# Two PSUM banks for the filling projections of a dilated attention, an earlier first conditioning sum, and layer 1 projections emitted between attention heads

## The chip, the cores and the metric

The kernel runs on one core of a Trainium2 chip. Its time is the device time of one execution in microseconds (us); lower is better. The kernel before was timed in three runs: 3086.98, 3095.9 and 3100.1 us, median 3095.9 us. The profile is of another execution, which took 3091.59 us.

## The reference, cut to what matters

A two-layer encoder works on 2048 tokens of width 1024 in float32. Layer 0 mixes tokens with a dilated window attention (A, 8 heads of 64) beside a differential attention over all tokens (B, 4 heads of 2 x 64); layer 1 uses a banded attention with grouped keys (C, 16 query heads on 4 key heads). Each layer has a silu gate path and an output projection, and its norm is shifted and scaled by sums over the conditioning vector `c`.

```
cs = silu(c)
for layer in range(2):
    shift, scale, gate = split(cs @ ada_w[layer] + ada_b[layer], 3)
    h = rms_norm(x, norm_g[layer]) * (1 + scale) + shift
    if layer == 0:
        qa, ka, va, qb, kb, vb, g = split(h @ ab_w_in)
        ya = dilated_mixture_attention(qa, ka, va)   # (window, dilation): (128,1), (512,4), (2048,16)
        yb = differential_attention(qb, kb, vb)      # softmax1 - lam*softmax2, all 2048 keys
        y = (concat(ya, yb) * silu(g)) @ ab_w_out
    else:
        q, k, v, g = split(h @ c_w_in)
        y = (banded_attention(q, k, v, half_window=128, sink) * silu(g)) @ c_w_out
    x = x + gate * y
return rms_norm(x, final_g)
```

## The kernel before, in words

Every float32 product of a projection is made of three fp32r matmuls: both operands are split into a high and a low part, and high x high, high x low and low x high are summed in one PSUM bank (`three`, L271). One piece of a projection (`proj_pieces`, L310) is 128 output columns for a block of 512 tokens, 24 such matmuls of 128x512. Its weights come in by one DMA, ScalarE and then VectorE or GpSimd split them (L319, L320), and a sink reads the finished bank: for the gates ScalarE takes a tanh (L385), VectorE multiplies (L387), and a DMA stores the result (`sink_gate`, L382).

The stages in the program's order are these. `layer0_proj` (L427) sums the products of `ada_w` with the conditioning vector (`ada_acc`, L152: eight products on VectorE for each of four sums `acc_ss`; four small matmuls with `ones` add up the partitions, L200), norms x, and makes q, k and v of B. `diff_attention` (L542) runs the four heads B0 to B3, and the projections of A stand in the program behind them. `dilated_attention` (L669) runs eight heads A0 to A7 in pairs; each head has a natural half (scores `pqn`, transposes `ptn`, output `pyn`) and a half by residue classes (`pqc`, `ptc`, `pyc`), and after each pair its two patterns are combined (`dil_combine`, L893: the factors are transposed into `pf`, L911, go to DRAM and come back broadcast as `F`, L922). Beside these heads a generator of 32 gate pieces (`layer0_gate_proj`, L537, tile `pp_g0` in bank `mm` of the pool `psG`) is advanced at every second `tick` (L719). `layer0_out` (L1010) multiplies attention and gate and projects; the part called 0b (L1197, tokens 768 to 1791, the upper half of the contraction) takes its tiles from `psG` too, the full part starts at L1209 in the pool `psO`. Layer 1 follows: `layer1_norm` and `layer1_qkv` for a block of 512 tokens, `attend` (L1092) for each of 16 tiles t of 128 queries (scores `pqC`, transposes `ptC`, output `pyC`), 32 gate pieces (`layer1_gate`, L1062, `pp_g1`), the output.

PSUM has eight banks in this plan. During the dilated heads `psG` holds one, `psA` holds s=2, t=3, y=2.

No queue is written by hand. The framework's scheduler sets the order of each engine's instructions before the program runs, from the program's order, the buffers that a tile may use and its own estimates of durations; so a piece that the program names late can stand early on an engine if its buffers are free, and the order is fixed on the chip.

## Time and profile before

| | |
|---|---|
| median of 3 runs | 3095.9 us (3086.98 to 3100.1) |
| profiled execution | 3091.59 us |
| its span | 3089.5 us |
| TensorE (PE) busy | 2789.2 us, 90% of the span |
| VectorE (DVE) busy | 1908.3 us, 62% |
| ScalarE (ACT) busy | 1490.5 us, 48% |
| GpSimd (POOL) busy | 1140.2 us, 37% |
| mean granted TensorE clock | 0.96 of 2.4 GHz |
| DMA | 593.78 MB, 192 GB/s |

The busy times are of one execution on the chip. A busy TensorE is a sum over the modelled ends of pipelined matmuls; how far apart two matmuls start says more. The granted clock is a mean over a stretch of the two levels 1.2 and 2.4 GHz, 1.00 being the upper one.

### The profile page before, as it was taken

The page shows a single profiled execution, that of the slowest core. Times are in us where ns is not written, and L with a number is a line of the kernel's source. Part 1 is how long each engine was busy: PE and PEld are TensorE (multiplying, and loading weights), DVE is VectorE, ACT ScalarE, POOL GpSimd, SP SyncE. Part 2 cuts the span into 40 slices and gives each one's busy share as a digit, 9 for nine tenths or more (in the row PEclk, how much of TensorE's full clock was granted, in tenths as well). Part 3 has the DMA queues.
Part 4 walks back from the last instruction along what each step waited for, and adds up shares of the span by engine and source line. Part 5 has one row for each costly group of instructions (what it writes and reads, how often), then busy time and mean ns, then how long its engine had stood idle before and what let it go on. Part 6 is the DMA issues. An engine that isn't in the chain of part 4 may idle for free. (4 is left out here: it accounts for less than half of the span.)

```text
span 3089.5 us, 43710 instructions
## 1 busy us (share of the span) xinstructions
PE 2789.2 (90%) x14992; PEld 2340.6 (76%) x14992; DVE 1908.3 (62%) x4128; ACT 1490.5 (48%) x2841; POOL 1140.2 (37%) x755
## 2 busy tenths in 40 slices
PE   4999899999999999998778885899888999999898
PEld 3788778888888888876666774788777778887687
DVE  7425286777677676657676665354565676565476
ACT  4311255555555555536666562122565576565321
POOL 3200075555655654312433432132333353333221
PEclk8999999999999999999889998999989999999999
DMA  6587743653654552357778986586988678885654
GB/s 261 207 297 233 206 137 110 188 174 112 169 157 159 152 167 86 133 169 203 179 197 214 254 225 195 189 289 196 254 203 228 182 177 209 215 220 180 206 196 160
DMA packets 554552, 593.78 MB, mean 192 GB/s; under 512 B 32257, under 2 KB 421594, under 8 KB 548186
## 3 DMA queue, kind: packets, MB, share of 16 engines
q1 hardware_dynamic: 542490, 574.21, 64.2%
q10 hardware_dynamic: 11840, 16.78, 1.7%
q8 instruction: 119, 1.95, 0.3%
q14 instruction: 103, 0.84, 0.1%
HBM read 414.36 MB, written 176.46 MB: 191 GB/s over the span
## 5 line engine op out<-in xcount | busy, mean ns | idle before, releaser
L615 ACT ACTIVATE s<-s,nm 128x2048 f32<-128x2048 f32 x128 | 257.0, 2008 | 170.3 <-DVE nm L614 170.2
L621 POOL TENSOR_SCALAR s<-s,rr 128x1536 f32<-128x1536 f32 x64 | 125.2, 1956 | 364.2 <-DVE rr L619 265.6
L564 PE MATMUL pq<-kB,q 128*128 128x512 f32 x512 | 215.9, 422 | 30.0 <-DMA kB<-kB 14.0
L1124 DVE CUSTOM_DVE_ANT_0 sC<-pqC,tabC,isl 128x384 f32<-128x384 f32 (+1 forms) x256 | 148.3, 597 | 134.5 <-PE pqC L565 91.7
L624 POOL TENSOR_TENSOR s<-s,s 128x1536 f32<-128x1536 f32 x64 | 229.0, 3579 | 4.8
L636 ACT ACTIVATE th<-pt 128x512 fp32r<-128x512 f32 x256 | 146.2, 596 | 171.0 <-PE pt L632 138.2
L609 DVE CUSTOM_DVE_ANT_0 s<-pq,ndist 128x1024 f32<-128x1024 f32 x128 | 156.0, 1219 | 93.4 <-PE pq L565 65.7
L565 PE MATMUL pq<-kB,q 128*128 128x512 f32 x512 | 206.5, 403 | 0.0
L637 DVE TENSOR_TENSOR tl<-pt,th 128x512 fp32r<-128x512 f32 x256 | 169.3, 682 | 55.8 <-ACT th L636 55.6
L609 DVE CUSTOM_DVE_ANT_0 s<-pq,ndist,mx 128x1024 f32<-128x1024 f32 x128 | 163.4, 1276 | 28.8 <-PE pq L565 26.8
L1132 ACT ACTIVATE sC<-sC,nmC 128x384 f32<-128x384 f32 (+1 forms) x256 | 151.6, 595 | 57.4 <-DVE nmC L1129 57.0
L276 PE MATMUL py<-tl,vB 128*128 128x256 f32 x512 | 150.2, 293 | 7.8 <-DVE tl L637 7.8
L632 PE MATMUL pt<-ident,s 128*128 128x128 f32 x1024 | 149.9, 275 | 0.0
L273 PE MATMUL py<-th,vB 128*128 128x256 f32 x512 | 147.1, 287 | 1.8 <-ACT th L636 1.7
L277 PE MATMUL py<-th,vB 128*128 128x256 f32 x512 | 145.3, 284 | 0.0
L564 PEld LDWEIGHTS pq<-kB,q 128*128 128x128 f32 x512 | 98.7, 193 | 59.6 <-DVE mx L609 23.6
L1138 PE MATMUL ptC<-ident,sC 128*128 128x128 f32 x736 | 136.4, 282 | 3.4 <-ACT sC L1132 3.4
L967 POOL TENSOR_TENSOR yr<-yr,gr 128x512 f32<-128x512 f32 (+1 forms) x46 | 58.0, 1262 | 214.6 <-DMA yr<-yT 56.9
L277 PE MATMUL pp_l<-h1T,wt_l 128*128 128x512 f32 x320 | 127.7, 401 | 8.6 <-POOL wt_l L320 6.5
L1145 POOL TENSOR_SCALAR hC<-rC 128x512 fp32r<-128x512 f32 x64 | 41.4, 646 | 239.2 <-ACT rC L1144 195.1
L273 PE MATMUL pp_l<-h1T,wt_l 128*128 128x512 f32 x320 | 127.7, 400 | 0.1
L276 PE MATMUL pp_l<-h1T,wt_l 128*128 128x512 f32 x320 | 127.3, 399 | 0.0
(415 smaller groups left out, 9118.3 us busy)
## 6 DMA issues: line engine op xcount, KB each, us to landing
wr_a<-in_ab_w_in_dram SPq DMA_DIRECT2D x48, 512.0 KB
wr_l<-in_c_w_in_dram SPq DMA_DIRECT2D x48, 512.0 KB
hD<-h0T SPq DMA_DIRECT2D x8, 2048.0 KB
aw_ss<-in_ada_w_dram SPq DMA_DIRECT2D x32, 512.0 KB
hs_a<-hD SPq DMA_DIRECT2D x16, 1024.0 KB
q<-qB SPq DMA_DIRECT2D x128, 128.0 KB
wr_g<-in_ab_w_in_dram SPq DMA_DIRECT2D x32, 512.0 KB
hs_g<-hD SPq DMA_DIRECT2D x16, 1024.0 KB
```

Source lines behind the costliest of these rows:

```text
L273: first = nc.tensor.matmul(pt, l[0], r[0], start=(k == 0), stop=False)
L276: nc.tensor.matmul(pt, l[0], r[1], start=False, stop=False)
L277: nc.tensor.matmul(pt, l[1], r[0], start=False, stop=(k == nk - 1))
L564: first = nc.tensor.matmul(ps_, q0, k0, start=True, stop=False)
L565: nc.tensor.matmul(ps_, q1, k1, start=False, stop=True)
L609: nc.vector.tensor_tensor_reduce(out=s_[:, half * 1024:(half + 1) * 1024], in0=pq, in1=ndist[:, o:o + 1024], scale=1.0, scalar=LOW if half ...
L615: nc.scalar.activation(s_, s_, AF.Exp, bias=nm, scale=slope_B(h), accum_out=lsum[:, a, t:t + 1])
L624: nc.gpsimd.tensor_tensor(Pm[0][:, W:], Pm[0][:, W:], Pm[1][:, W:], op=OP.add)
L632: nc.tensor.transpose(pt[:, kk, j], A[j][:, kb * P:(kb + 1) * P], ident)
L637: nc.vector.tensor_tensor(lo, src, f32(hi), op=OP.subtract)
L1124: nc.vector.tensor_tensor_reduce(out=s_[:, :n], in0=pq[:, :n], in1=tab[:, o:o + n], scale=1.0, scalar=isl[:, h:h + 1], op0=OP.add, op1=OP.max,
L1132: nc.scalar.activation(Sx[r][:, :n], Sx[r][:, :n], AF.Exp, bias=nm[:, h:h + 1], scale=slope_C(h), accum_out=ls[:, h:h + 1])
```

## The change

There are three edits.

1. A class `Turns` hands out tiles from several pools, one after the other. The gate pieces of the dilated attention and part 0b of the output take their tiles in turn from `psG` and from a new pool `psF` of one bank, which is opened with the pools of A. The transposes of A have two banks, not three.
2. Of the eight products of each first conditioning sum, the third and fourth (`OWN`) are no longer made on VectorE: TensorE multiplies the raw weight columns by the conditioning values and adds them in the bank that sums the partitions. The load of `ada1_1` is issued ahead of the first weights of q.
3. In layer 1 `layer1_qkv` of the next block and 24 of the 32 gate pieces are generators now, advanced inside `attend` after each group of four heads; the norm of the next block stands ahead of the attends instead of behind them. The last eight gate pieces follow after the attends as before, behind the last scores.

```diff
+class Turns:
+    def __init__(self, *pools):
+        self.pools, self.n = pools, 0
+    def tile(self, *args, **kw):
+        self.n += 1
+        return self.pools[self.n % len(self.pools)].tile(*args, **kw)
...
+    OWN = (2, 3)
...
             for k in range(KC):
-                add(acc, raw[:, k], k)
+                if k not in OWN:
+                    add(acc, raw[:, k], k)
...
-            for f in range(4):
-                nc.tensor.matmul(pc[:, f:f + 1], accs[i, j][:, f * P:(f + 1) * P], ones[:, 0:1], start=True, stop=True)
+            terms = [(accs[i, j], ones[:, 0:1])]
+            if raw is not None:
+                terms = [(raw[i][j][:, k], cs[:, k:k + 1]) for k in OWN] + terms
+            for n, (a, b) in enumerate(terms):
+                for f in range(4):
+                    nc.tensor.matmul(pc[:, f:f + 1], a[:, f * P:(f + 1) * P], b, start=(n == 0 and f == 0),
+                                     stop=(n == len(terms) - 1), skip_group_check=True)
...
             ada_load(raw, 0, 0)
+            ada_load(raw, 0, 1, (1,))
             w0 = load_w(pool, ab_w_in, 1536, CH, "qb0", "wt", nc.gpsimd)
-            ada_load(raw, 0, 1)
+            ada_load(raw, 0, 1, (0,))
...
-        ps = Bufs(ps_, s=2, t=3, y=2)
+        ps = Bufs(ps_, s=2, t=2, y=2)
...
-        dilated_attention(pool_A, pool_AC, ps_A, fill, psG)
+        psG2 = Turns(psG, Bufs(with_A.enter_context(psum("psF", side="right")), mm=1))
+        dilated_attention(pool_A, pool_AC, ps_A, fill, psG2)
...
-        layer0_out(pool, psG, w, [upper], g, x, x0d, "0b", "mm", range(FULL, HALF))
+        layer0_out(pool, psG2, w, [upper], g, x, x0d, "0b", "mm", range(FULL, HALF))
...
+            ts = range(max(4 * b - 1, 0), 4 * b + 3 if b < TB - 1 else NT)
             if b + 1 < TB:
                 h1 = layer1_norm(pj, psj, b + 1)
-                layer1_qkv(pj, psj, h1, b + 1, qs)
+                between, n = layer1_qkv(pj, psj, h1, b + 1, qs), 14
+            else:
+                between, n = chain(*(layer1_gate(pj, psj, h1 if g == TB - 1 else None, g)
+                                     for g in (TB - 1, *range(TB - 2)))), 8 * (TB - 1)
+            at = [0, 0]
+            def tick():
+                at[0] += 1
+                while at[1] * len(ts) * C_KV < at[0] * n:
+                    at[1] += 1
+                    next(between, None)
+            for t in ts:
+                last = attend(pool, ps, t, V, consts, tick)
+            for _ in between:
+                pass
```

The order of the engines moves with it at three places. The first is ScalarE late in the last differential head, B3; `th3_6` are its copies of transposed scores of query pair 6, `s3_14` and `s3_15` the exponentials of tiles 14 and 15, `th_g0` the tanh of a gate piece and `wt_g0` the split of its weights. Before:

```order
L615 ACTIVATE s3_15_0_9628,l3_8116<-s3_15_0_9628,nm3_15_0_9642 128x2048
L385 ACTIVATE th_g04_1_14755<-pp_g0_1_4_14730 128x512
L319 ACTIVATE wt_g0_1_6_15109<-wr_g0_1_6_15107 128x1024
L641 ACTIVATE yB3_8115<-py3_5_9247 128x256
L636 ACTIVATE th3_6_0_9467<-pt3_6_0_9462 128x512
L645 ACTIVATE sq3_2_9369<-yB3_8115 128x512
L636 ACTIVATE th3_6_1_9482<-pt3_6_1_9477 128x512
L615 ACTIVATE s3_15_1_9645,l3_8116<-s3_15_1_9645,nm3_15_1_9659 128x2048
L649 ACTIVATE row3_2_9373<-pr3_2_9371 1x512
L385 ACTIVATE th_g05_1_14916<-pp_g0_1_5_14891 128x512
L319 ACTIVATE wt_g0_1_7_15314<-wr_g0_1_7_15312 128x1024
```

and now:

```order
L658 ACTIVATE th3_6_0_9491<-pt3_6_0_9486 128x512
L658 ACTIVATE th3_6_1_9506<-pt3_6_1_9501 128x512
L637 ACTIVATE s3_14_0_9612,l3_8140<-s3_14_0_9612,nm3_14_0_9626 128x2048
L671 ACTIVATE row3_2_9397<-pr3_2_9395 1x512
L637 ACTIVATE s3_14_1_9629,l3_8140<-s3_14_1_9629,nm3_14_1_9643 128x2048
L658 ACTIVATE th3_6_2_9521<-pt3_6_2_9516 128x512
L658 ACTIVATE th3_6_3_9536<-pt3_6_3_9531 128x512
L637 ACTIVATE s3_15_0_9652,l3_8140<-s3_15_0_9652,nm3_15_0_9666 128x2048
L658 ACTIVATE th3_6_4_9551<-pt3_6_4_9546 128x512
L658 ACTIVATE th3_6_5_9566<-pt3_6_5_9561 128x512
L637 ACTIVATE s3_15_1_9669,l3_8140<-s3_15_1_9669,nm3_15_1_9683 128x2048
```

The gate pieces are gone from this place. In the whole program 480 of the 768 gate matmuls of layer 0 stood ahead of the first dilated score on TensorE, and 48 do now; the other 720 stand in the dilated heads A0 to A3 (A2's class half has none), where before the heads A0 to A7 held 288, most of them from A5's class half on.

The second is TensorE at the end of the last dilated pair; `pyc7` and `ptc7` are of head A7, `pf3` is the transpose of the last combining factors, `po0b_6_1` the second half of output tile 6 of part 0b. Before:

```order
L277 MATMUL po0b_6_1_18575<-woh0b_18540,yl0b_6_4_18582 128x512
L875 MATMUL pyc7_3_18392<-cl7_3_2_18410,vc7_3_18366 128x512
L875 MATMUL pyc7_3_18392<-ch7_3_0_18419,vc7_3_18366 128x384
L875 MATMUL pyc7_3_18392<-cl7_3_0_18420,vc7_3_18366 128x384
L911 MATMUL pf3_18491<-ident_110,M3_18477 64x128
L875 MATMUL pyc7_3_18392<-ch7_3_3_18431,vc7_3_18366 128x384
L875 MATMUL pyc7_3_18392<-cl7_3_3_18432,vc7_3_18366 128x384
L273 MATMUL po0b_7_0_18618<-woh0b_18540,yh0b_7_4_18625 128x512
L276 MATMUL po0b_7_0_18618<-wol0b_18541,yh0b_7_4_18625 128x512
L277 MATMUL po0b_7_0_18618<-woh0b_18540,yl0b_7_4_18626 128x512
```

and now:

```order
L294 MATMUL po0b_10_0_18771<-woh0b_18567,yh0b_10_4_18778 128x512
L897 MATMUL pyc7_3_18419<-cl7_3_2_18437,vc7_3_18393 128x512
L883 MATMUL ptc7_3_3_18454<-ident_110,scl7_3_1_18402 128x128
L883 MATMUL ptc7_3_3_18454<-ident_110,scl7_3_2_18408 128x128
L883 MATMUL ptc7_3_3_18454<-ident_110,scl7_3_3_18414 128x128
L297 MATMUL po0b_10_0_18771<-wol0b_18568,yh0b_10_4_18778 128x512
L298 MATMUL po0b_10_0_18771<-woh0b_18567,yl0b_10_4_18779 128x512
L933 MATMUL pf3_18518<-ident_110,M3_18504 64x128
L294 MATMUL po0b_10_1_18772<-woh0b_18567,yh0b_10_4_18778 128x512
L297 MATMUL po0b_10_1_18772<-wol0b_18568,yh0b_10_4_18778 128x512
```

Ahead of `pf3` stood 24 of the 192 matmuls of part 0b, the tile 6; now 108 do, the tiles 6 to 9 and half of 10.

The third is TensorE at the start of the last attend of layer 1, t = 15; `pp_g1_1_7` is the last piece of gate block 1. Before:

```order
L1138 MATMUL ptC15_0_15_26855<-ident_110,sC15_0_26821 128x128
L1138 MATMUL ptC15_0_15_26855<-ident_110,sC15_1_26826 128x128
L1138 MATMUL ptC15_0_15_26855<-ident_110,sC15_2_26831 128x128
L1138 MATMUL ptC15_0_15_26855<-ident_110,sC15_3_26836 128x128
L273 MATMUL pp_g1_1_7_27950<-h1G1_0_5_27673,wt_g1_1_7_27947 128x512
L276 MATMUL pp_g1_1_7_27950<-h1G1_1_5_27681,wt_g1_1_7_27947 128x512
L1151 MATMUL pyC15_0_26843<-hC15_0_14_26849,vC_14_26223 128x512
L277 MATMUL pp_g1_1_7_27950<-h1G1_0_5_27673,wt_g1_1_7_27947 128x512
L273 MATMUL pp_g1_1_7_27950<-h1G1_0_6_27674,wt_g1_1_7_27947 128x512
```

and now:

```order
L1160 MATMUL ptC15_0_15_27647<-ident_110,sC15_0_27613 128x128
L1160 MATMUL ptC15_0_15_27647<-ident_110,sC15_1_27618 128x128
L1160 MATMUL ptC15_0_15_27647<-ident_110,sC15_2_27623 128x128
L1160 MATMUL ptC15_0_15_27647<-ident_110,sC15_3_27628 128x128
L1173 MATMUL pyC15_0_27635<-hC15_0_14_27641,vC_14_26633 128x512
L1173 MATMUL pyC15_0_27635<-lC15_0_14_27642,vC_14_26633 128x512
L586 MATMUL pqC15_8_27788<-khC15_27597,qC_15_27599 128x256
L587 MATMUL pqC15_8_27788<-klC15_27598,qC_15_27599 128x256
L586 MATMUL pqC15_9_27793<-khC15_27597,qC_15_27599 128x256
L587 MATMUL pqC15_9_27793<-klC15_27598,qC_15_27599 128x256
```

The pieces that the program lets run here have ended before: about a quarter of t = 14's and all of t = 15's attention matmuls, some 100, now stand without gate matmuls between them, and the last eight pieces follow the last scores as before.

## Rows read from the trace of the kernel before

**Rows 1.** the page: busy time by engine, and the granted clock in 40 slices.

```profile
PE 2789.2 (90%) x14992; PEld 2340.6 (76%) x14992; DVE 1908.3 (62%) x4128; ACT 1490.5 (48%) x2841; POOL 1140.2 (37%) x755
...
PEclk8999999999999999999889998999989999999999
```

**Rows 2.** busy time by engine in nine stretches of layer 0.

```profile
core 0: us, PE busy (x) PEld busy (x) DVE busy (x) ACT busy (x) POOL busy (x), PEclk, DMA share, GB/s
1181.60:1242.80 61.20, 61.20 (x345) 52.35 (x345) 41.21 (x76) 33.68 (x47) 26.95 (x10) 1.00 0.28 80
1242.80:1375.50 132.70, 125.60 (x679) 104.65 (x678) 73.96 (x136) 58.32 (x85) 44.03 (x20) 0.99 0.47 152
1451.20:1476.60 25.40, 21.18 (x120) 17.43 (x118) 17.57 (x55) 16.90 (x42) 6.09 (x8) 0.93 0.71 182
1476.60:1510.00 33.40, 21.68 (x129) 17.81 (x129) 20.84 (x66) 19.61 (x55) 15.46 (x15) 0.88 0.73 183
1510.00:1536.10 26.10, 20.78 (x108) 16.55 (x107) 18.95 (x47) 19.54 (x50) 14.85 (x16) 0.89 0.67 173
1674.70:1710.20 35.50, 32.96 (x174) 27.34 (x173) 20.20 (x58) 20.40 (x48) 9.96 (x11) 1.00 0.90 262
1710.20:1752.40 42.20, 36.66 (x198) 30.90 (x199) 28.92 (x71) 24.88 (x60) 11.60 (x10) 0.92 0.93 254
1752.40:1802.00 49.60, 44.67 (x209) 35.31 (x208) 28.63 (x56) 26.07 (x60) 30.07 (x26) 0.93 0.82 212
1868.20:1947.10 78.90, 43.97 (x153) 31.86 (x151) 38.01 (x49) 11.31 (x15) 11.55 (x7) 0.85 0.73 213
```

**Rows 3.** TensorE's timeline: gate matmuls back to back, first and fifth.

```profile
1342.64 0.39 PE L276 MATMUL pp_g<-hs_g,wt_g 128*128 128x512 f32 x1
...
1343.55 0.39 PE L277 MATMUL pp_g<-hs_g,wt_g 128*128 128x512 f32 x1
```

**Rows 4.** groups by line of VectorE between 1181.6 and 1242.8 us.

```profile
L320 DVE TENSOR_TENSOR wt_g<-wr_g,wt_g 128x1024 fp32r<-128x1024 f32 x3 | 3.7, 1223 | 0.3 <-ACT wt_g L319 0.3
L387 DVE SCALAR_TENSOR_TENSOR gg_g<-th_g,pp_g 128x512 f32<-128x512 f32 x5 | 3.4, 684 | 4.5 <-ACT th_g L385 4.5
```

**Rows 5.** groups by line of TensorE in the same stretch.

```profile
L276 PE MATMUL pp_g<-hs_g,wt_g 128*128 128x512 f32 x40 | 15.7, 392 | 0.0
```

**Rows 6.** what TensorE waited for, 1330 to 1880 us.

```profile
PE pqc L564 <- DMA kc<-kA: 10.0, 7, 3.9
...
PE pp_g L273 <- DVE gg_g L387: 3.2, 1, 3.2
...
PE ptc L861 <- ACT cr L868: 2.4, 3, 1.9
```

**Rows 7.** what TensorE waited for between 1868.2 and 1947.1 us.

```profile
PE po0b L273 <- DVE xo0b L991: 34.4, 12, 9.7
```

**Rows 8.** the timeline of VectorE: the last weight split of layer 0's output.

```profile
1914.38 1.23 DVE L942 TENSOR_TENSOR wol0a<-wor0a,woh0a 128x1024 fp32r<-128x1024 f32 x1 [3.67 <-ACT woh0a L941]
```

**Rows 9.** the timeline of the start, three engines.

```profile
18.63 0.75 DVE L160 SCALAR_TENSOR_TENSOR acc_ss<-ada,cs,acc_ss 128x512 f32<-128x512 f32 x1
...
26.31 1.06 ACT L265 ACTIVATE wh_qb<-wr_qb 128x1024 fp32r<-128x1024 f32 x1 [9.71 <-DMA wr_qb<-in_ab_w_in_dram]
...
51.35 1.87 PE L200 MATMUL pc<-ones,acc_ss 128*128 128x1 f32 x8 [4.06 <-DVE acc_ss L160]
...
53.08 0.77 PE L273 MATMUL pp_qb<-h0T,wh_qb 128*128 128x512 f32 x1
```

**Rows 10.** busy time by engine in layer 1's attends 3, 7 and 11.

```profile
2299.00:2334.00 35.00, 26.86 (x120) 20.38 (x119) 24.29 (x71) 23.65 (x53) 17.22 (x15) 0.80 0.75 192
2467.40:2500.50 33.10, 26.76 (x128) 19.10 (x128) 29.83 (x77) 27.64 (x65) 17.39 (x16) 0.90 0.66 152
2632.40:2676.60 44.20, 44.20 (x227) 37.02 (x226) 27.71 (x65) 29.30 (x67) 18.04 (x13) 1.00 0.72 172
```

More of the change, by code (lines that the diff above doesn't have):

```diff
@@ L3 @@
 from functools import partial
+from itertools import chain
 import concourse.bass as bass
@@ L215, in ada_steps, with ada_load @@
         return [(partial(sums, i, j), partial(rest, i, j)) for j in range(2) for i in which]
-    def ada_load(tiles, l, j):
-        for i in (1, 0):
+    def ada_load(tiles, l, j, parts=(1, 0)):
+        for i in parts:
             for n in range(2):
@@ L1059, in layer1_qkv, with layer1_gate @@
         pieces += [(f * P, sink_heads(pool, q_rows(f), qs[:, f:f + 1], f"qc{f}"), None) for f in range(8)]
-        proj_block(pool, ps, c_w_in, h, b, pieces, "l1")
-    def layer1_gate(pool, ps, h, b, after):
+        return proj_pieces(pool, ps, c_w_in, h, b, pieces, "l1")
+    def layer1_gate(pool, ps, h, b, after=lambda b, n: None):
         if h is None:
@@ L1068, in layer1_gate @@
                     nc.sync.dma_start(f32(h[i][k]), hD1[b, i, :, k])
-        proj_block(pool, ps, c_w_in, h, b, [(D + 2 * CH + f * P,
-                                             sink_gate(pool, lambda b, f=f: G1[b][f * P:(f + 1) * P], f"g1{f}"), None)
-                                            for f in range(8)], "g1", after)
+        yield from proj_pieces(pool, ps, c_w_in, h, b, [(D + 2 * CH + f * P,
+                                                        sink_gate(pool, lambda b, f=f: G1[b][f * P:(f + 1) * P], f"g1{f}"),
+                                                        None) for f in range(8)], "g1", after)
     def layer1_consts(pool):
@@ L1090, in layer1_consts, with attend @@
         return tab, nsl, isl, sk
-    def attend(pool, ps, t, V, consts):
+    def attend(pool, ps, t, V, consts, tick):
         tab, nsl, isl, sk = consts
@@ L1158, in attend @@
                     py[:64].rearrange("p (g a q) -> p a g q", a=2, q=P)[:, a], op=OP.add)
+            tick()
         d = sm.tile([P, C_H], F32, name=f"dC{t}", tag="dC", bufs=2)
@@ L1210, in tile_encoder @@
             h1 = layer1_norm(pj, psj, 0)
-            layer1_qkv(pj, psj, h1, 0, qs)
+            for _ in layer1_qkv(pj, psj, h1, 0, qs):
+                pass
             ps_ = Bufs(ps_, o=5)
@@ L1220, in tile_encoder @@
         for b in range(TB):
-            for t in range(max(4 * b - 1, 0), 4 * b + 3 if b < TB - 1 else NT):
-                last = attend(pool, ps, t, V, consts)
+            ts = range(max(4 * b - 1, 0), 4 * b + 3 if b < TB - 1 else NT)
             if b + 1 < TB:
                 h1 = layer1_norm(pj, psj, b + 1)
-                layer1_qkv(pj, psj, h1, b + 1, qs)
+                between, n = layer1_qkv(pj, psj, h1, b + 1, qs), 14
[11 more added lines that the diff above has]
+            for _ in between:
+                pass
         mid = range(K2, K2 + 2)
@@ L1230, in tile_encoder @@
         raw = Bufs(pool, alias=dict(wor="yh"), yh=4)
-        for b in (TB - 1, *range(TB - 1)):
-            layer1_gate(pj, psj, h1 if b == TB - 1 else None, b,
-                        lambda b, n: last if (b + 1) % TB * 8 + n >= 8 * TB - 8 else None)
+        for _ in layer1_gate(pj, psj, None, TB - 2, lambda b, n: last):
+            pass
         last2 = range(K2 + 2, KC)
```

## The prediction

> **What bounds the kernel now.** I read the page first: TensorE is busy for 90% of the span, the next engine for 62%, and in the slices the granted clock falls only at the start, in the dilated attention and near layer 1's start [rows 1]. So time is to be had where TensorE idles or runs at the lower level, and the next view is the busy time by stretch [rows 2]. Three kinds of stretch show there. In the differential head B3 with gate pieces between its work, TensorE is busy all of 61.2 us at clock 1.00. The dilated half-heads without gate pieces (A1's class half at 1451.2, A2's natural half at 1476.6 and class half at 1510.0) take 25.4, 33.4 and 26.1 us with TensorE idle for a fifth to a third of it and a clock of 0.88 to 0.93; the long one follows the end of a pair. The half-heads with gate pieces (A5's class half at 1674.7, A6's natural half at 1710.2 and class half at 1752.4) take 35.5, 42.2 and 49.6 us. From the waits the reader is to see that a dilated half-head waits for its own DMAs and neighbours, and that the gate piece's single bank, the thing the first edit doubles, held TensorE for only 3.2 us [rows 6], while it cost part 0b of the output 34.4 us [rows 7].
>
> **Unit prices.** Five gate matmuls start within 0.91 us, so one costs 0.228 us of TensorE [rows 3]. The quarter of B3 from 1181.6 holds 118 of them (one of their three lines stands in [rows 5]: 40 + 39 + 39), 26.9 us; what is left of its 61.2 us is 34.3. VectorE's 41.2 us less 7.1 for gates leaves 34.1 [rows 2, 4]. Without gate pieces neither engine lets this quarter go below 34.
>
> **Edit 1a, the gate pieces leave B3.** The second bank exists only once B's own banks are given back, and the pieces take the two banks in turn, so the order keeps 48 of the 480 gate matmuls that stood in B3. 432 x 0.228 = 98.5 us of TensorE goes from there. What is late next is the pair of engines with 34 us of work each, which wait for one another. I take 41 us for a bare quarter: at 34.3 nothing is lost, and at the 77% that TensorE is busy in attend 3 of layer 1, which has no projections beside it [rows 10], it would be 44.5. How many such quarters are laid bare: the stretch from 1242.8 lasts 132.7 us and holds 295 gate matmuls (counted in the order), 67.3 us; the other 65.4 us are 1.9 quarters of 34.3, and with the quarter at 1181.6 that makes 2.9 [rows 2]. 2.9 x (41 - 34.3) = 19.4 us is lost, and about 1 us at the end of the head, where nothing covers the last pair any more. Gain 98.5 - 20 = 78 us; from 60 (2.9 x 10.2 = 30, and 10 at the end, rounded) to 95.
>
> **Edit 1b, they arrive in the dilated heads.** A0 to A3 receive them; A4 to A7, which had most of theirs, run bare. By rows of before a gate matmul added (35.5 - 25.4) / 70 = 0.144 us in A5's class half, (42.2 - 33.4) / 72 = 0.122 in A6's natural half, both ends of a pair's start, and (49.6 - 26.1) / 90 = 0.261 in A6's class half (70, 72 and 90 counted in the order). The median is 0.144, the mean weighted by matmuls 0.183. I take 0.165 between them: 432 x 0.165 = 71 us; from 53 to 113 by the ends. The DMA share there is 0.82 to 0.93 against 0.67 to 0.73 bare [rows 2], which is why I do not take the low end. One transposes bank fewer: the wait that names such a bank was 2.4 us in all with three [rows 6]; I charge 3 us, between 0 and 9 (1 us in each of nine bare half-heads).
>
> A rule of the Trainium skill bears on the turns: its page "Perfetto Trace Analysis", section "Matmuls", says that independent matmul groups should rotate through PSUM banks, so that the evacuation of one overlaps the next group. The 3.2 us of rows 6 say that for the gate pieces there is next to nothing to overlap, and the 34.4 us of rows 7 agree with it for part 0b.
>
> **Edit 1c, part 0b.** With one bank each half tile waited for VectorE to empty it: 78.9 us from the last factors to the full output part, for 44.0 us of TensorE at clock 0.85 [rows 2, 7]. Now 108 instead of 24 matmuls stand ahead of the factors, and the rest has two banks. What is late next are the weights of the lower half, whose last split stands at 1914.38 [rows 8], 33 us before the full part began (1947.1); it needs the queue of ScalarE, which also issues the factor loads. The 84 matmuls that move ahead cost 84 x 0.144 = 12 us in the last class half, some 5 us of upper halves fill the wait for weights. 33 - 12 + 5 = 26, rounded to a gain of 25 us; from 10 to 34.
>
> **Edit 2, the start.** Eight products of 0.75 us leave VectorE [rows 9], 6 us in all. The first projection matmul started at 53.08, right behind the last sum's matmuls at 51.35, which it stood behind in TensorE's queue; now that last sum stands behind 17 projection matmuls, so they may begin when their first operands are there. The 32 matmuls that replace the products cost TensorE time that was idle. Against it: the q weights' DMA is behind 2 MB more. ScalarE waited for them to 26.31 [rows 9]; later weights hold GpSimd, whose queue has the weight split ahead of h. I take a gain of 5 us, since VectorE is busy almost without a break there and gets 6 us less; from -2 (the weights decide) to 12 (the whole advance of TensorE is kept).
>
> **Edit 3, layer 1.** Before, the scheduler had already put projections between attention matmuls; attends 3 and 7 were bare of them with 35.0 and 33.1 us for 94 and 99 attention matmuls and 24 to 28 of the norm's transposes, some 0.33 us for one. Attend 11 with 117 gate matmuls took 44.2 us, (44.2 - 26.7) / 110 = 0.159 [rows 10]. In the new order the bare places behind the norms stay (half an attend earlier), and some 100 attention matmuls of t = 14 and 15 become bare: 100 x 0.17 = 17 us. The pieces missing there stand in attends 0 to 9, 54 more than before, which the idle parts can take; I credit 7. Cost 10 us; from -5 to 25.
>
> **The sum.** -78 + 71 + 3 - 25 - 5 + 10 = -24 us against the profiled execution's 3091.6 us (a span of 3089.5 and 2.1 around it): 3067.6. That execution lies 4.3 us under the median of the three runs, so the time to be compared with it is 3072 us, 0.8% less than 3095.9. By the bounds taken one at a time the likeliest case's own range is 3045 to 3098.
>
> **Rivals.** The change does not do what its name says (the fill gets a second bank but loses its place in B3) in all cases; what differs is the price.
> First, the dilated heads pay full price. Every moved matmul costs the 0.261 us of A6's class half: 113 us instead of 71, so +18 and with the median's distance 3114 us, slower by 0.6%. The place is A0 to A3, whose own loads of keys and values share the DMA queues with 6 times the gate pieces; it decides where the wait for `kc` and its like, 10.0 us in all before [rows 6], grows by more than 40 us. The DMA share of 0.93 in A6's natural half speaks for it; the low price there, at that share, speaks against it.
> Second, the stalls of the dilated heads swallow the pieces at 0.122 us: 53 us instead of 71, 3054 us. The idle fifth to third of the bare half-heads speaks for it; the 0.261 against.
> Third, the ends of layer 1 pay: 25 instead of 10, and the start gains nothing: 3092 us, no change.
> Fourth, the clock. Where pieces alternate between banks TensorE could pause often enough to fall to its lower level: the bare pair start at 1476.6 shows a clock of 0.88 against 0.92 to 1.00 with pieces [rows 2], so the trace speaks against it. At 0.78 of the speed the 720 matmuls would take 720 x 0.228 x 0.28 = 46 us more: 3118 us. The Trainium skill has such a case on its page "TensorE: Matmul & The Clock Gate", section "A second HAM failure mode: psum-queue depth-cycling", which says that cycling through PSUM banks left small idle times that took the clock down again and again; the filled rows do not show it so far.
>
> **How the numbers follow.** The sum's case gets 0.48, the full price 0.22, the swallowed pieces 0.18, the layer 1 case 0.08, the clock 0.04. About 0.5%, 15 us, is what a measurement can tell from no change: the limits are 3080 and 3111. The first case is faster with 0.33, within with 0.14, slower with 0.01; the second 0.10 within and 0.12 slower; the third 0.17 faster and 0.01 within; the fourth 0.06 within and 0.02 slower; the clock slower. Together 0.50 faster, 0.31 the same, 0.19 slower. The range that leaves out a tenth on each side is 3035 to 3118.
>
> **What would show it.** Right: the quarters of B3 without gates at 38 to 45 us and busy for 75 to 90% of it on TensorE; the filled half-heads of A0 to A3 at 43 to 50 us with a DMA share near 0.9; A4 to A7 as bare as A1 and A2 are now; no wait of `po0b` on its own bank over a few us; the first q matmul near 40 us; t = 15 with TensorE idle. Wrong: bare quarters of B3 at 50 us or more, filled half-heads over 52 us, or a full output part that starts no earlier behind the last factors.

## The result and the profile after

The changed kernel takes 3055.28 us (median of 4 runs, 3048.72 to 3058.63) against 3091.44 us of the kernel before in the same session (4 runs, 3082.36 to 3100.1): ratio 0.9881, 95% interval 0.9845 to 0.9917. In a later session with more runs it was 0.9889 (0.9869 to 0.9909). The forecast was 3072 us, range 3035 to 3118, faster with 0.50. The profiled execution took 3054.5 us with a span of 3052.5, 37.0 us less than before.

First the page, as in [rows 1]:

```profile
PE 2797.3 (92%) x15056; PEld 2351.4 (77%) x15056; DVE 1894.7 (62%) x4120; ACT 1491.3 (49%) x2841; POOL 1147.5 (38%) x755
...
PEclk9999899999999999999999998999999999999999
```

TensorE is busy for 8 us longer and the span is 37 us shorter, so idle time went. In the line of the granted clock the 8s of the dilated heads (slices 20, 21 and 25 before) are gone, and slices 5 and 28 have one now; a slice of 76 us is too coarse to show more. The busy time by stretch does (columns as in [rows 2]). The stretches are cut at the first matmul of a stage: up to the first scores of B0; up to B3's second quarter of scores; B3's other three quarters; the dilated heads up to A7's class half; from there to the full output part (this holds part 0b); and the rest. Before:

```profile
0.00:374.50 374.50, 316.97 (x1782) 273.32 (x1782) 166.69 (x321) 99.34 (x157) 55.22 (x53) 0.95 0.70 240
374.50:1117.10 742.60, 708.91 (x4261) 614.51 (x4262) 533.21 (x981) 410.53 (x557) 432.24 (x197) 0.98 0.51 150
1117.10:1375.50 258.40, 244.58 (x1363) 207.55 (x1363) 167.75 (x306) 126.34 (x177) 98.38 (x40) 0.99 0.44 143
1375.50:1830.40 454.90, 372.97 (x2037) 307.16 (x2036) 295.53 (x833) 288.45 (x741) 153.16 (x154) 0.91 0.80 207
1830.40:1947.10 116.70, 75.88 (x315) 55.81 (x313) 70.53 (x127) 39.60 (x83) 31.73 (x28) 0.88 0.71 211
1947.10:3089.50 1142.40, 1069.91 (x5240) 882.24 (x5240) 674.56 (x1562) 526.21 (x1128) 369.48 (x283) 0.97 0.74 207
```

After:

```profile
0.00:369.20 369.20, 329.82 (x1845) 287.56 (x1845) 162.68 (x313) 99.34 (x157) 54.05 (x53) 0.97 0.72 244
369.20:1105.30 736.10, 707.94 (x4262) 612.73 (x4263) 529.60 (x981) 410.10 (x557) 434.06 (x197) 0.98 0.52 151
1105.30:1282.40 177.10, 155.31 (x932) 131.90 (x932) 146.44 (x280) 98.28 (x140) 75.36 (x31) 0.94 0.26 81
1282.40:1808.10 525.70, 459.39 (x2453) 379.30 (x2452) 317.46 (x861) 317.03 (x779) 175.66 (x163) 0.94 0.83 219
1808.10:1903.90 95.80, 75.96 (x356) 59.47 (x354) 66.45 (x126) 37.24 (x79) 27.67 (x27) 0.93 0.84 244
1903.90:3052.50 1148.60, 1068.84 (x5216) 880.45 (x5216) 672.04 (x1562) 529.34 (x1131) 380.70 (x284) 0.97 0.74 208
```

The third row lost 81.3 us, the fourth gained 70.8, the fifth lost 20.9, the first two lost 11.8, the last gained 6.2. That is -37.0 in all. The two large terms, the move of the gate pieces, nearly cancel: 10.5 us of gain are left of them.

The second fence answers to [rows 2]: a quarter of B3, three half-heads with gate pieces (A0's class half, A1's natural and class half), a bare pair (A4 and A5), and the eight half-heads A0 to A3 together, seven of them with gate pieces.

```profile
1158.80:1206.80 48.00, 42.94 (x249) 35.51 (x248) 39.32 (x72) 28.93 (x39) 21.18 (x8) 0.93 0.10 23
1315.70:1367.70 52.00, 48.09 (x238) 38.76 (x237) 25.88 (x58) 28.67 (x64) 15.83 (x13) 0.97 0.95 272
1367.70:1409.90 42.20, 42.20 (x242) 36.91 (x241) 24.71 (x63) 26.64 (x61) 14.03 (x9) 1.00 0.77 209
1409.90:1462.30 52.40, 47.36 (x239) 39.48 (x237) 27.71 (x70) 27.47 (x60) 14.36 (x14) 0.97 0.86 244
1626.10:1731.40 105.30, 85.25 (x476) 68.38 (x476) 75.92 (x222) 75.00 (x199) 41.88 (x46) 0.93 0.84 206
1282.40:1626.10 343.70, 313.79 (x1641) 262.12 (x1639) 188.94 (x482) 188.58 (x437) 99.13 (x83) 0.96 0.82 227
```

The quarter without gates takes 48.0 us instead of 61.2, at clock 0.93 instead of 1.00, with TensorE idle for 5 us; A1's natural half runs at clock 1.00 without a gap; the bare pair has TensorE idle for 20 of 105 us. The waits at part 0b's banks, 34.4 us in [rows 7], are now these (line, what it waited for, us in total, times, longest):

```profile
PE po0b L294 <- DVE xo0b L1013: 6.6, 1, 6.6
PE po L294 <- DVE xo0b L1013: 5.2, 1, 5.2
```

In the fifth row TensorE is busy as long as before (75.96 and 75.88 us) and its idle time fell from 40.8 to 19.8 us. From the transpose of the last factors (`pf`, before and after) to the full part it was 77.8 us, and is 39.0 now (1864.89 to 1903.9):

```profile
1869.26 0.27 PE L911 MATMUL pf<-ident,M 128*64 128x128 f32 x1
```

```profile
1864.89 0.27 PE L933 MATMUL pf<-ident,M 128*64 128x128 f32 x1
```

And the start, against [rows 9] (start, us, engine, line, operation):

```profile
31.73 1.06 ACT L286 ACTIVATE wh_qb<-wr_qb 128x1024 fp32r<-128x1024 f32 x1 [0.33 <-DMA wr_qb<-in_ab_w_in_dram]
...
45.46 0.77 PE L294 MATMUL pp_qb<-h0T,wh_qb 128*128 128x512 f32 x1
```

The first q matmul starts at 45.46 instead of 53.08, though the weights arrive 5.4 us later (31.73 against 26.31).

### The profile page after: what moved, and what is told of

Read it like the earlier page. It is cut to its first block, busy times and chain, and to the rows that moved or that the text cites. A ratio compares the mean times of both kernels' runs of the same rounds, so it can differ in the third digit from the quotient of the medians.

```text
span 3052.5 us, 43787 instructions
## 1 busy us (share of the span) xinstructions
PE 2797.3 (92%) x15056; PEld 2351.4 (77%) x15056; DVE 1894.7 (62%) x4120; ACT 1491.3 (49%) x2841; POOL 1147.5 (38%) x755
## 5 line engine op out<-in xcount | busy, mean ns | idle before, releaser
L297 PE MATMUL py<-tl,vB 128*128 128x256 f32 x512 | 152.4, 298 | 14.7 <-DVE tl L659 13.8
L341 POOL TENSOR_TENSOR wt_g<-wr_g,wt_g 128x1024 fp32r<-128x1024 f32 x32 | 77.1, 2408 | 182.8 <-ACT wt_g L340 177.5
L294 PE MATMUL pp_l<-h1T,wt_l 128*128 128x512 f32 x320 | 129.0, 404 | 7.3 <-ACT wt_l L340 6.8
L298 PE MATMUL pp_l<-h1T,wt_l 128*128 128x512 f32 x320 | 129.0, 405 | 5.4 <-POOL wt_l L341 3.4
```

The costliest lines, as they stand in the source:

```text
L294: first = nc.tensor.matmul(pt, l[0], r[0], start=(k == 0), stop=False)
L297: nc.tensor.matmul(pt, l[0], r[1], start=False, stop=False)
L298: nc.tensor.matmul(pt, l[1], r[0], start=False, stop=(k == nk - 1))
```

## The experiments

Two theories stood after the result. The first is the prediction's bookkeeping: moving the gate pieces out of B3 is nearly a wash, and what edit 1 wins, it wins by part 0b's second bank; edit 3 costs some 10 us. The rival says that the stages hide it: the pieces' move is worth something by itself, or edits 2 and 3 carry the gain. A second question was the price of a gate matmul in the dilated heads. Twelve kernels ran, in three sessions with a median of before of 3084.75, 3087.61 and 3093.43 us. The table gives the ratio to before (95% interval) and, from one trace each, the time up to B0's scores, from there to B3's second quarter, of B3's other three quarters, from the first dilated score to the full output part, and from there to the end. A single profile lies up to 11 us off its kernel's median, so the stages are compared, and the totals by the ratio. In the table "t=2" stands for two transposes banks in the dilated heads, and "one piece a half" for one gate piece in each half-head.

| kernel | ratio | start | B | B3 | A and 0b | rest |
|---|---|---|---|---|---|---|
| before | 1 | 374.5 | 742.6 | 258.4 | 571.6 | 1142.4 |
| edit 1 alone | 0.9915 (0.9891-0.9940) | 375.0 | 741.0 | 175.8 | 603.8 | 1156.2 |
| edit 2 alone | 0.9992 (0.9975-1.0009) | 367.8 | 736.1 | 258.2 | 581.8 | 1143.2 |
| edit 3 alone | 0.9955 (0.9939-0.9971) | 376.1 | 741.1 | 260.9 | 566.5 | 1134.5 |
| edits 1 and 2 | 0.9898 (0.9870-0.9925) | 369.4 | 737.6 | 177.7 | 620.1 | 1139.0 |
| changed, again | 0.9889 (0.9869-0.9909) | 367.9 | 733.4 | 177.7 | 621.8 | 1147.2 |
| only t=2 | 0.9976 (0.9965-0.9987) | 376.7 | 739.4 | 259.8 | 560.3 | 1145.7 |
| t=2, 0b two banks | 0.9892 (0.9875-0.9909) | 376.9 | 742.1 | 259.1 | 537.5 | 1142.8 |
| t=2, gates two banks | 0.9879 (0.9864-0.9894) | 374.3 | 745.2 | 175.8 | 615.9 | 1147.3 |
| one piece a half, 20 in B3 | 0.9875 (0.9855-0.9895) | 368.3 | 736.5 | 256.2 | 537.2 | 1144.4 |
| one piece a half, 16 in B3 | 1.0005 (0.9991-1.0019) | 367.2 | 738.9 | 234.9 | 602.9 | 1148.7 |
| the 20, fewer weight loads | 0.9805 (0.9792-0.9819) | 369.5 | 734.8 | 240.4 | 531.7 | 1157.1 |
| 0b two banks, edits 2 and 3 | 0.9834 (0.9816-0.9853) | 369.4 | 739.0 | 258.8 | 533.6 | 1141.5 |

**The edits one by one.** Edit 1 alone:

```diff
-        ps = Bufs(ps_, s=2, t=3, y=2)
+        ps = Bufs(ps_, s=2, t=2, y=2)
...
-        dilated_attention(pool_A, pool_AC, ps_A, fill, psG)
+        psG2 = Turns(psG, Bufs(with_A.enter_context(psum("psF", side="right")), mm=1))
+        dilated_attention(pool_A, pool_AC, ps_A, fill, psG2)
...
-        layer0_out(pool, psG, w, [upper], g, x, x0d, "0b", "mm", range(FULL, HALF))
+        layer0_out(pool, psG2, w, [upper], g, x, x0d, "0b", "mm", range(FULL, HALF))
```

> Edit 1 alone on the kernel before: two banks in turns for the gate pieces and part 0b, two transposes banks. Here the order spreads the gate pieces to A4 (B3 keeps 48) and starts part 0b in A5 already. If the prediction's parts hold (B3 gives 78, the heads take 71 to 77, part 0b gives 25), it is 25 to 35 us faster than before, and the dilated heads' and part 0b's stretch together is about 50 us longer while B3's is 81 shorter. Rival: the gain of the changed kernel is mostly edits 2 and 3; then edit 1 alone is within 15 us of before.

The ratio, 0.9915, is 26 us, as expected. The stages are not: B3 gives 82.6 us, but the heads and part 0b take 32 instead of 50, since the scheduler spreads the pieces to A4 and puts 192 matmuls of part 0b from A5 on; and the rest takes 13.8 us more. The wait of TensorE for the split `yh` in the first 102.6 us of the full output part, before and with part 0b's tiles done early, shows where:

```profile
PE po L273 <- ACT yh L970: 4.4, 4, 2.2
```

```profile
PE po L284 <- ACT yh L981: 20.9, 4, 14.4
```

The split runs on ScalarE, whose queue holds the loads of the last factors (`F`), the lower half's weights and, before the later splits, layer 1's weights (`wt_l`) ahead of it (start, us, engine, line, operation, in brackets the idle time before and what ended it; ACTq are the DMA issues):

```profile
1899.91 1.20 ACTq L951 DMA_DIRECT2D wor0a<-in_ab_w_out_dram  x2
...
1906.75 4.59 ACTq L933 DMA_DIRECT2D F<-fA  x6
1911.39 2.00 ACT L952 ACTIVATE woh0a<-wor0a 128x1024 fp32r<-128x1024 f32 x2 [14.04 <-DMA F<-fA]
...
1916.13 0.63 ACT L981 ACTIVATE yh<-yr 128x512 fp32r<-128x512 f32 x1 [2.73 <-DVE y L938]
...
1925.42 1.06 ACT L952 ACTIVATE woh0a<-wor0a 128x1024 fp32r<-128x1024 f32 x1 [2.42 <-DMA wor0a<-in_ab_w_out_dram]
1933.86 1.06 ACT L330 ACTIVATE wt_l<-wr_l 128x1024 fp32r<-128x1024 f32 x1 [7.38 <-DMA wr_l<-in_c_w_in_dram]
...
1936.61 1.13 ACT L981 ACTIVATE yh<-yr 128x512 fp32r<-128x512 f32 x2
```

The longest wait, 14.4 us, ends behind the `yh` of 1916.13. So between the last factors and a full part that runs without waits lies a chain on that queue, and part 0b, done in earlier heads, is not there to fill it. That this wait alone makes the 13.8 us is not shown: the kernel with one piece a half and twenty in B3 waits 20.6 us there, and its rest is 1144.4.

Edit 2 alone:

```diff
+    OWN = (2, 3)
...
-                add(acc, raw[:, k], k)
+                if k not in OWN:
+                    add(acc, raw[:, k], k)
...
+            ada_load(raw, 0, 1, (1,))
             w0 = load_w(pool, ab_w_in, 1536, CH, "qb0", "wt", nc.gpsimd)
-            ada_load(raw, 0, 1)
+            ada_load(raw, 0, 1, (0,))
```

> Edit 2 alone on the kernel before. The prediction's part: the first projection matmul starts some 5 us earlier and everything behind it, 5 us in all. Rival, from the changed kernel's trace, where the first head's scores came 5.3 us earlier and B3 12 us earlier: edit 2 gives 12 us, the rest through the heads of B. Third: the clock of B0 and B1 differs between executions and the 6.5 us are of the execution, not of the edit; then the second stretch shows nothing here.

The time is that of before, and yet the trace shows the 12 us of the rival: the first two stretches are 6.7 and 6.5 us shorter. They are so in all eight kernels with edit 2 (367 to 370 and 733 to 739 us) against the six without (374 to 377 and 739 to 745). What gives them back here is the order behind it: the scheduler lays the last gate pieces otherwise, into A6's natural half and A7, and from the first dilated score to the full part this kernel takes 10.2 us more than before:

```profile
0.00:367.80 367.80, 328.41 (x1845) 286.37 (x1846) 162.59 (x313) 99.05 (x157) 54.01 (x53) 0.97 0.72 245
367.80:1103.90 736.10, 707.79 (x4262) 612.43 (x4263) 530.22 (x981) 409.70 (x557) 433.74 (x197) 0.98 0.52 151
1362.10:1943.90 581.80, 449.77 (x2349) 365.23 (x2347) 360.12 (x959) 326.81 (x823) 179.60 (x182) 0.89 0.76 204
```

TensorE's busy time there is as before (449.8 us against 373.0 + 75.9): the 10 us are idle time.

Edit 3 alone, the projections in generators advanced between head groups, and the norm ahead of them:

```diff
-            for t in range(max(4 * b - 1, 0), 4 * b + 3 if b < TB - 1 else NT):
-                last = attend(pool, ps, t, V, consts)
             if b + 1 < TB:
                 h1 = layer1_norm(pj, psj, b + 1)
-                layer1_qkv(pj, psj, h1, b + 1, qs)
+                between, n = layer1_qkv(pj, psj, h1, b + 1, qs), 14
...
+            for t in ts:
+                last = attend(pool, ps, t, V, consts, tick)
```

> Edit 3 alone on the kernel before: layer 1's projections mixed between groups of heads. The prediction charges 10 us (range -5 to 25): the stretch from the full output part to the end grows from 1142 us, and the changed kernel's trace shows 1149 for it, so 6 to 10 us slower. Rival: the norms put ahead and mixed pieces gain in the attends (691 against 701 us there) and the loss stands at the ends for another reason; then this kernel is the same or faster.

The rival was right: 14 us faster. The stretch is cut here at the scores of t = 14:

```profile
1944.60:2783.30 838.70, 795.62 (x4023) 662.55 (x4024) 476.39 (x1107) 421.59 (x919) 291.89 (x223) 0.97 0.81 219
2783.30:3079.10 295.80, 271.32 (x1218) 218.94 (x1216) 190.84 (x455) 102.14 (x210) 79.34 (x60) 0.97 0.56 181
```

Before, the two parts take 819.6 and 322.8 us. 141 of layer 1's projection matmuls left the end (235 of 376 are left there), which gets 27.0 us shorter, 0.19 us for each; ahead of it they cost 19.1 us, 0.136 each. On top of edits 1 and 2 the order of layer 1 comes out otherwise. Edits 1 and 2 without edit 3:

```diff
-                between, n = layer1_qkv(pj, psj, h1, b + 1, qs), 14
+                layer1_qkv(pj, psj, h1, b + 1, qs)
```

> The changed kernel without edit 3 (layer 1 as before). Its order up to the output of layer 0 is the changed kernel's. If edit 3 costs 6 to 10 us, this is 6 to 10 us faster than the changed kernel, near 3047 us, 1.4% under before. Rival: edit 3 is neutral, and this kernel is at 3055.

> The changed kernel itself, for a comparison on one chip. By the stages of the traces edit 3 costs 9 to 10 us on top of edits 1 and 2 (1148.6 against 1139.0 us from the full output part to the end); then this run is 5 to 10 us above edits 1 and 2, about 0.988 to 0.992 of before. Rival: edit 3 is worth on top of them the 14 us that it was worth alone; then it is 0.985 of before.

(The changed kernel ran again unaltered.) In the traces edit 3 adds 8 to 10 us to the rest, 1148.6 and 1147.2 us against 1139.0. That is one trace without it; in the ten kernels without edit 3 the rest lies between 1139.0 and 1157.1, so this difference settles nothing. The ratios, 0.9889 and 0.9898, don't show it either; their difference is -0.1% with some 0.35% to either side. So edit 3 gains alone, and whether it gains or loses in the changed kernel is not settled.

**What in edit 1 wins.** Three kernels take it apart; all have two transposes banks. Only that:

```diff
-        ps = Bufs(ps_, s=2, t=3, y=2)
+        ps = Bufs(ps_, s=2, t=2, y=2)
```

> Only the third transposes bank of the dilated heads is taken away; nothing uses the bank. The prediction charged 3 us (0 to 9). Beside the run with part 0b on two banks this differs in the bank of part 0b alone, and its gate pieces stand at the same places. If part 0b's gain needs its second bank, this run is 0 to 10 us slower than before; if the new order alone lets part 0b run early, it gains 10 us or more.

Then part 0b alone in turns:

```diff
-        dilated_attention(pool_A, pool_AC, ps_A, fill, psG2)
+        dilated_attention(pool_A, pool_AC, ps_A, fill, psG)
```

> Edit 1 without the turns of the gate pieces: part 0b has two banks, the transposes two, the gate pieces one as before, so B3 keeps its 480 gate matmuls. If moving the pieces out of B3 is near a wash (81 us gained there, 77 paid in the heads by the changed kernel's trace) and the 27 us come from part 0b's second bank, this is 20 to 30 us faster than before, as much as edit 1 alone, with B3 at 258 us and the stretch from the first dilated score to the full output part near 545. Rival: part 0b gains only because the pieces have left the last heads; then the gain is under 10 us.

And the gate pieces alone:

```diff
-        layer0_out(pool, psG2, w, [upper], g, x, x0d, "0b", "mm", range(FULL, HALF))
+        layer0_out(pool, psG, w, [upper], g, x, x0d, "0b", "mm", range(FULL, HALF))
```

> Edit 1 without part 0b: the gate pieces take two banks in turn and leave B3, part 0b has one bank, the transposes two. If moving the pieces is near a wash, B3 is 177 us (before 258), the stretch from the first dilated score to the full output part about 650 (before 572), and the time within 10 us of before. Rival: moving the pieces out of B3 is itself worth 20 us or more.

The first came out a little faster than before (0.9976), not slower. It is not before's order with a bank less: its last gate matmul starts at 1708.2 us, in A5's natural half, where before's stands in A7's at 1814.6, and part 0b starts at 1751.0 instead of 1835.0. So what the bank itself costs is not separated. The second came as expected. The third refutes the wash for a kernel with one bank for part 0b: it is as fast as the changed kernel. By ratio the gates' turns are worth 1.0% on top of two transposes banks, part 0b's 0.8%, and both together, edit 1, 0.6%, no more than either.

On top of part 0b's second bank, then, the wash holds: the gates' turns make no kernel faster there. Without them the ratio is 0.9892, with them 0.9915 (edit 1); with edits 2 and 3 beside, it is 0.9834 without (the last kernel of the table) and 0.9889 with them (the changed kernel). The two win in part the same thing. The waits of part 0b on its bank, from A7's class half to the full part, with neither, with part 0b's second bank, and with the gates' alone:

```profile
PE po0b L273 <- DVE xo0b L991: 18.4, 6, 8.1
```

```profile
PE po0b L284 <- DVE xo0b L1002: 1.8, 1, 1.8
```

```profile
PE po0b L284 <- DVE xo0b L1002: 12.1, 5, 8.2
```

Part 0b needs the finished gates of its tokens. Where the gates are done by A4, 60 of its 192 matmuls stand in A5 to A7's natural half (9 with neither) and the others beside A7's class half, and one bank makes TensorE wait for 12 us, not 18 or 34. Against the kernel with neither, the move of the gate pieces takes 84.0 us from B3 and adds 77.8 up to A7's class half; the stretch from there to the full part is 22.2 us shorter:

```profile
1836.60:1936.20 99.60, 71.39 (x323) 55.03 (x321) 64.18 (x122) 37.59 (x77) 24.32 (x25) 0.89 0.71 209
```

```profile
1833.80:1911.20 77.40, 62.71 (x296) 48.76 (x294) 51.75 (x105) 31.00 (x69) 19.11 (x21) 0.92 0.71 203
```

Early gates alone do not move part 0b: in the changed kernel they end in A3 and yet all 192 matmuls stand beside A7's class half, since the scheduler laid them there. Up to the full part part 0b's second bank wins 23.5 us over the kernel with neither (796.6 against 820.1 us for B3, the heads and 0b), the gates' turns 28.4 (791.7) and both 40.5 (779.6). So most of the two gains do add up to there; with both, the rest takes 10.5 us more, where the queue shown above stands.

The Trainium skill's rule on turns through PSUM banks ("Perfetto Trace Analysis", section "Matmuls") agrees with the first two of these waits of part 0b, 18.4 against 1.8 us. For the gate pieces the gain isn't that overlap: their own wait at the bank was 3.2 us in [rows 6] and is 1.9 us in the changed kernel's heads.

**The price in the dilated heads.** The gate pieces have one bank again; twenty (or sixteen) are emitted ahead of the heads, and an order rule on TensorE holds the first matmul of each other one behind a score of its half-head (the mark):

```diff
+        gate = layer0_gate_proj(fill, psf, lambda b, n: C.get("mark"))
+        for _ in range(20):
+            next(gate)
...
-            if steps[0] % 2 == 0:
-                next(gate, None)
+            for _ in range(1 if steps[0] % 4 == 1 else 0):
+                next(gate, None)
...
-                    scores(pq[:, j], q, KH[:, c0:c0 + 256], q, KL[:, c0:c0 + 256])
+                    C["mark"] = scores(pq[:, j], q, KH[:, c0:c0 + 256], q, KL[:, c0:c0 + 256])
```

> Edits 1 and 2, but the gate pieces have one bank again, twenty of them run in B3 as before, and the other twelve are held back by an order rule to one per dilated half-head (24 matmuls in each from A0's natural half to A5's class half); part 0b keeps two banks. If the idle fifth to third of a bare half-head takes the first 24 matmuls for less than 0.08 us each, the stretch from the first dilated score to the full output part is 510 to 525 us (before 572, changed kernel 622) with B3 at 258, and the time is 15 to 30 us under that of edits 1 and 2. If a matmul costs the same 0.165 however thin the pieces stand, that stretch is 540 to 550 and the time equals edits 1 and 2.

> The same with sixteen pieces in B3 and one in each of the sixteen half-heads. Four pieces more leave B3 (96 matmuls at the 0.19 us that each gave there, 18 us); the heads pay under 8 us for them if thin filling is cheap, 16 if not. Against it: part 0b of the output can start only when the last pieces are stored, so its tiles all stand behind A7. I expect a time within 10 us of the run with twenty.

The kernel with twenty takes 537.2 us there, 3 us under the linear price's case and as much as with part 0b's two banks alone (537.5). The rows of its twelve half-heads with 24 gate matmuls each, to be held against the bare pair and the filled A0 to A3 of the changed kernel above:

```profile
1361.00:1745.40 384.40, 317.54 (x1677) 256.46 (x1675) 233.84 (x675) 234.41 (x596) 117.50 (x119) 0.91 0.80 204
1390.40:1745.40 355.00, 294.93 (x1558) 237.08 (x1557) 213.08 (x611) 219.72 (x557) 115.15 (x118) 0.91 0.80 202
```

Three bare pairs would be 3 x 105.3 = 315.9 us; these three take 384.4, so 288 matmuls cost 68.5 us, 0.238 each; in the run with sixteen the same half-heads take 379.9 us, 0.222 each. That is TensorE's own 0.228, as far as single traces tell. TensorE is idle for 66.9 us in them, 22 a pair, as in a bare pair (20). The filled pairs of the changed kernel are idle for 29.9 us in two, 15 a pair. Thin pieces fill no idle time here; dense ones fill a little.

With sixteen in B3 my expectation missed by 40 us: the last pieces end in A7's class half, and the 192 matmuls of part 0b stand behind it all, 98.8 us at clock 0.80:

```profile
1845.10:1943.90 98.80, 69.94 (x242) 51.65 (x241) 61.14 (x86) 24.54 (x45) 25.69 (x23) 0.80 0.74 231
```

Whether the pieces' DMAs make them dear was asked by leaving out weight loads:

```diff
-                wr = pool.tile([P, KC, P], F32, name=f"wr_{name}_{b}_{n}", tag="wraw", bufs=2)
-                nc.sync.dma_start(wr, w[:, c0:c0 + P].rearrange("(k p) f -> p k f", p=P))
+                if name != "g0" or n == 0:
+                    wr = pool.tile([P, KC, P], F32, name=f"wr_{name}_{b}_{n}", tag="wraw", bufs=2)
+                    nc.sync.dma_start(wr, w[:, c0:c0 + P].rearrange("(k p) f -> p k f", p=P))
```

> The run with one piece per half-head, with the gate weights loaded only for the first of the eight pieces of a token block (the other seven use the same weights, so the gates are not the reference's): 28 of 32 loads of 512 KB are left out, eleven of the twelve that fell into the dilated heads. There 24 matmuls cost about 0.24 us each. If they cost it because the pieces' loads share the DMA queues with the heads' keys and values, 5.8 MB less at some 240 GB/s take 24 us from the 384 us between A0's natural half and A5's class half. If the price is TensorE's time and the waits between the engines, the stretch stays within 8 us of 384.

```profile
1379.60:1725.00 345.40, 286.09 (x1571) 231.20 (x1571) 212.08 (x613) 218.92 (x559) 113.86 (x117) 0.94 0.74 192
```

Two more pieces stand in A0's natural half here, so the stretch from A0's class half is compared: 345.4 us against 355.0. That is 9.6 us of the 24 that the DMA theory asked, at a DMA share of 0.74 instead of 0.80. But the run with sixteen has the same pieces in the same eleven half-heads, with all their loads, and takes no longer:

```profile
1375.40:1720.90 345.50, 291.17 (x1565) 236.72 (x1563) 209.75 (x605) 218.59 (x552) 116.72 (x119) 0.92 0.80 203
```

So this stretch doesn't show that the loads make the pieces dear. The kernel with fewer loads is 0.7% faster all the same (0.9805 against 0.9875), with two pieces moved from B3 to A0; over B3's other three quarters and the twelve half-heads, which hold all 768 gate matmuls in both, it takes 620.7 us against 640.6. How much of that is the loads and how much the order stays open, and so does what keeps a pair's 20 us idle.

**A version that beats both.** Part 0b alone on two banks, gate pieces on one, edits 2 and 3 as in the change:

```diff
-        dilated_attention(pool_A, pool_AC, ps_A, fill, psG2)
+        dilated_attention(pool_A, pool_AC, ps_A, fill, psG)
```

> Part 0b alone on two banks (the gate pieces on one), with edits 2 and 3. From the single runs: 0.989 for part 0b, 11 us from edit 2 where the order of the heads doesn't give it back, 8 to 14 from edit 3 alone: 0.984 of before, 15 us under the changed kernel. If the gains do not add (edit 3 lost 10 us of the traces on top of edits 1 and 2), it is 0.988 to 0.989, the same as the changed kernel.

It is 1.7% faster than before (0.9834), and against the changed kernel's 0.9889 some 0.55% (17 us) faster, with 0.28% to either side; the two were compared through the kernel before, not in one session, and by their medians alone (3043.73 and 3053.43) it is 10 us.

```profile
0.00:369.40 369.40, 328.21 (x1846) 286.28 (x1846) 162.71 (x313) 99.14 (x157) 53.96 (x53) 0.97 0.72 243
1108.40:1367.20 258.80, 246.58 (x1363) 209.42 (x1363) 165.66 (x306) 125.95 (x177) 99.31 (x40) 0.97 0.44 142
1367.20:1810.90 443.70, 373.06 (x2036) 301.12 (x2035) 300.90 (x835) 289.49 (x745) 154.33 (x155) 0.93 0.85 215
1367.20:1900.80 533.60, 442.36 (x2373) 357.26 (x2371) 362.47 (x957) 323.36 (x818) 178.18 (x180) 0.92 0.83 217
1900.80:3042.30 1141.50, 1062.85 (x5216) 878.25 (x5216) 673.48 (x1563) 529.11 (x1133) 375.41 (x286) 0.97 0.74 210
```

It keeps edit 2's start, B3 with its gates (258.8 us), and takes 533.6 us from the first dilated score to the full part, 88 less than the changed kernel for 82 more in B3. Up to A7's class half it takes 443.7 us there against 525.7, again 82, so between these two traces the move of the pieces is a wash. In the first 102.6 us of its full part TensorE still waits for `yh`:

```profile
PE po L294 <- ACT yh L992: 21.1, 3, 17.1
```

## Why the prediction was right

The forecast's case held. Its terms against the traces: gates out of B3, -78, measured -81.3. The heads with one transposes bank fewer, +74, measured +70.8 up to A7's class half. Part 0b, -25, measured -20.9. The start, -5, measured -11.8. Layer 1, +10, measured +6.2. The sum of -24 became -37.0: all terms but part 0b's came out better, by 3 to 7 us each. The measured 3055 lies at the second rival's 3054 and not at the case's 3072, but the heads' price, below, says that this is chance.

The price of a bare quarter in B3 was the most uncertain large term. For B3's last two parts the forecast's loss was 20 us. Measured: 388 gate matmuls less are 88.5 us of TensorE, the two stretches got 70.3 us shorter (193.9 to 123.6), so 18 us was lost. The single quarter at 1158.8 took 48.0 us and not the 38 to 45 that I named, but 247 of B3's own matmuls stand in it and not 227; for 227 it would be 44.

The price of a moved matmul, taken as 0.165 us between 0.122 and 0.261, came out as 70.8 / 432 = 0.164. This is a mean that hides two things: 696 matmuls added in A0 to A3 cost 137.7 us, 0.198 each (343.7 us against 206.0, 1375.5 to 1581.5 before), and 264 taken from A4 to A7 gave 66.9 back, 0.253 each (248.9 us against 182.0). That the rows of before with the highest price (A6's class half, 0.261) were those being emptied was in the profile, and I averaged over it.

The first rival, the full price of 0.261, fell: the waits for `kc`, 10.0 us before, are 7.5 now (A0 to A3 hold 720 gate matmuls where they held 24, which is 30 times and not the 6 that I wrote). The second, that the idle parts swallow the pieces, fell harder, by the runs with one piece a half-head: 0.238 and 0.222. The third came partly: the rest grew by 6.2 us, but the start gained. The fourth fell: the filled heads run at 0.96, the bare pair at 0.93. Of the signs that I named, one of being wrong was touched: A0's and A1's class halves, with 110 and 117 gate matmuls, took 52.0 and 52.4 us, where over 52 was to speak against me. That the full part would start no earlier behind the last factors did not come.

Three steps were wrong or too narrow within the right sum. The start was mis-sized: the first q matmul came 7.6 us earlier, not the dozen us that its advance to 40 would be, yet nearly all of it reached the first scores, and another 5 to 6 us came in the heads of B, for which I had no term; where in B they come from was not tested. The transposes bank, charged with 3 us, shows no cost: the kernel without it is at 0.9976, though in another order. And my account of part 0b was too narrow. In the changed kernel its cause holds: TensorE's idle time there fell by 21.0 us and the wait at the bank by 22.6 (34.4 to 6.6 and 5.2), and on top of the second bank the pieces' move is the wash that I took it for. But I had no term for a kernel without that bank, and there the run with the gates' turns alone wins as much in part 0b's stretch. That the lower half's weights and ScalarE's queue are late next, which I named, showed in edit 1 alone and in the last kernel of the table, where 20.9 and 21.1 us are waited there. Layer 1's term has the right sign in the changed kernel's traces, at 6.2 of 10 us, and the wrong sign alone (-7.9 us in the trace, 14 by the ratio); on top of the other edits it is not settled.

## What to carry to other kernels

When filler work moves between stages, price it per instruction at the place that it leaves and at the place that it enters, and then ask what was waiting for its last piece: here that follower, part 0b, gave 20.9 of the 37.0 us, and the move itself 10.5. Two remedies that shorten the same stretch need not add (0.8% and 1.0% alone, 0.6% together); test each without the other before keeping both, since here the simpler one with the other edits beat the whole change. Where a scheduler lays the order, a small edit far ahead can cost or give 10 us behind it, so compare stage by stage.

## What the runs showed of the hardware

TensorE's idle time in the dilated heads did not shrink when one gate piece was put into each half-head: 22 us a pair against 20 bare, and the pieces cost 0.222 to 0.238 us a matmul, their full TensorE time of 0.228. B3's quarter without gates ran at a granted clock of 0.93 with TensorE idle for 5 of 48 us, where the filled quarter had 1.00 throughout. Taking 28 loads of 512 KB out of the gates (14.7 MB of 594) made a kernel 0.7% faster (0.9805 against 0.9875), but its order changed too, and the eleven half-heads with fewer loads took 345.4 us where another kernel with all its loads took 345.5.
